# A hybrid attention block: pools that wait tile by tile, later value loads, and a reordered start

## The chip, the cores and the metric

The kernel runs on one core of a Trainium2 chip. The metric is the device time of one execution in microseconds (us); the median of three runs before the change is 946.88 us (944.96 to 947.32). The engines are TensorE (PE, with its weight loads shown apart as PEld), VectorE (DVE), ScalarE (ACT), GpSimd (POOL) and SyncE (SP), which here issues every DMA. Each engine works through its own instructions in the order in which they stand.

## The reference

Input x has 1024 rows of 1024 float32 values. It is normalized and projected onto 6152 columns; these feed two attention branches, two gate paths and a merge:

```python
h = rms_norm(x, g_pre[l], NORM_EPS)
proj = jnp.einsum('bsd,dn->bsn', h, w_in[l])
qa, ka, va, fa, za, qb, kb, vb, zb, gates = jnp.split(proj, SPLIT_POINTS, axis=-1)
...
ya = fox_attention(split_heads(qa, FOX_HEADS), split_heads(ka, FOX_HEADS),
                   split_heads(va, FOX_HEADS), log_f)
ya = merge_heads(ya) * jax.nn.silu(za)
qd = apply_rope(...); kd = apply_rope(...)
yb = diff_attention(qd, kd, vd, lam)
yb = rms_norm(yb, g_subln[l], SUBLN_EPS) * (1.0 - lam_init)
yb = merge_heads(yb) * jax.nn.silu(zb)
gate_a, gate_b = jnp.split(jax.nn.sigmoid(gates), N_BRANCHES, axis=-1)
merged = (gate_a * jnp.einsum('bsw,wd->bsd', ya, w_branch[l, 0])
          + gate_b * jnp.einsum('bsw,wd->bsd', yb, w_branch[l, 1]))
y = jnp.einsum('bsd,de->bse', merged, w_out[l])
x = x + rms_norm(y, g_post[l], NORM_EPS)
```

The forgetting attention (fox) has 8 heads of 64 and adds a running sum of log forget gates to its logits. The differential attention has 4 heads, each the difference of two softmaxes, with rotated queries and keys (rope). Both are causal.

## The kernel before

Most operands are split in two: a rounded high part (`hi`) and the rest (`lo`), so that a product is three matmuls (hi·hi, hi·lo, lo·hi). A cast makes `hi`, a subtraction makes `lo`.

**Start and value projection** (lines 125 to 223). `g_row` is loaded and spread over 128 partitions by a matmul with ones (`gbc`), and ACT copies the two halves to `g_bc`. `x_block(i)` loads 128 rows of x (`xs`), squares and sums them on ACT, forms the scale `rs` on POOL, multiplies by scale and gain on DVE (`xg`), transposes on PE (`xt`), and splits into `hT`; the first block goes in two halves. `load_wv(k)` loads 128 rows of the value weights (`wvraw`) and splits them into `wvhi` and `wvlo`: casts on POOL, except the first half tile on DVE, and subtractions on DVE. `v_block(i)` multiplies (`pv`), and writes the values to DRAM (`vb_d`, `va_d`).

**Attention** (lines 251 to 651). Eight units follow: 0 to 3 differential, 4 to 7 fox. `unit_proj` projects keys and queries in halves (`pk`, `pq`). In units 0 to 3 `rope` copies the result out of PSUM on ACT (`rawk`, `rawq`), which frees its PSUM buffer, fetches the swapped halves by four DMAs (`swk`, `swq`), and combines them on DVE and POOL (`cosT`, `sinT`); `stack` splits into `KA`, `KB`, `TA`, `TB`. `swapped` makes the exchanged query tiles `X0` and `X1` by two DMAs each. `s_row` multiplies a row block of scores (`Sd`, `Sf`) with `TA`/`TB` and then with `X0`/`X1`, takes the row maximum on DVE (`mxd`, `mxf`), and the exponential on ACT. `av` transposes the probabilities and multiplies by the values `V`, loaded from DRAM, 1 MB for each unit. Projections of the next unit, the gate paths (`pz`), and other work are laid between the groups of a unit as filler. The lambda vectors `lt` are loaded at the beginning of this part.

**Gates, merge, output** (lines 654 on). Gate columns are projected (`pg`, then in a scheme with seven products `x_g`, with operands `T` loaded from DRAM), the branches are multiplied (`pb`), merged, and multiplied by the output weights (`x_o`).

**What sets the order.** The code is traced in program order and a scheduler places the instructions of each engine by a simulated timeline, so a small edit can move rows far from it. Tiles come from pools: a pool of a later part lies over the memory of a closed one. Before the change such a tile waits until the whole earlier pool is done with; PSUM pools as well. A tag with `bufs=n` has n slots that are used in turn.

Of the kernel before, what the change touches and what calls it, by code (L numbers as in the profile page):

```python
# [9 lines left out]
F32 = mybir.dt.float32  # L10
F32R = mybir.dt.float32r
AF = mybir.ActivationFunctionType
ALU = mybir.AluOpType
# [28 lines left out]
def f32(ap):  # L42
    return ap.bitcast(F32)
# [3 lines left out]
def tile_hybrid_block(  # L47
# [71 lines left out]
    with ExitStack() as st:  # L119
# [19 lines left out]
        def load_wv(k):  # L139
            raw = xp.tile([P, 1032], F32, tag="wvraw", name=f"wvraw{k}", bufs=4)  # L140
            nc.sync.dma_start(raw[:, 0:512], w[k * P:(k + 1) * P, VB:VB + 512])
            nc.sync.dma_start(raw[:, 512:1032], w[k * P:(k + 1) * P, VA:VA + 520])
            wv_hi[k] = vw.tile([P, 1032], F32R, name=f"wvhi{k}")
            wv_lo[k] = vw.tile([P, 1032], F32R, name=f"wvlo{k}")
            for a, b in ((0, 512), (512, 1032)):
                if k == 0 and a == 0:
                    nc.vector.tensor_copy(wv_hi[k][:, a:b], raw[:, a:b])
                else:
                    nc.gpsimd.tensor_scalar(
                        wv_hi[k][:, a:b], raw[:, a:b], 1.0, 1.0, op0=ALU.mult, op1=ALU.mult)  # L150
                nc.vector.tensor_tensor(
                    wv_lo[k][:, a:b], raw[:, a:b], wv_hi[k][:, a:b], op=ALU.subtract)

        def x_block(i):
            xs = wpool.tile([P, D], F32, tag="wraw", name=f"xs{i}")
            xg = xp.tile([P, D], F32, tag="xg", name=f"xg{i}", bufs=2)
            ss = small.tile([P, 1], F32, tag="ss", name=f"ss{i}")
            rs = small.tile([P, 1], F32, tag="rs", name=f"rs{i}")
            if i == 0:
                for half, acc in enumerate((rs, ss)):  # L160
                    hs = slice(half * CH, (half + 1) * CH)
                    nc.sync.dma_start(xs[:, hs], x2[0:P, hs])
# [88 lines left out]
    with ExitStack() as st:  # L251
        qk = st.enter_context(tc.tile_pool(name="qk", bufs=2))
        pp = st.enter_context(tc.tile_pool(name="pp", bufs=6))
        ptp = st.enter_context(tc.tile_pool(name="ptp", bufs=3))
        stg = st.enter_context(tc.tile_pool(name="stg", bufs=2))
        pj = st.enter_context(tc.tile_pool(name="pj", bufs=2, space=PSUM))
        sps = st.enter_context(tc.tile_pool(name="sps", bufs=3, space=PSUM))
        tps = st.enter_context(tc.tile_pool(name="tps2", bufs=2, space=PSUM))
        yps = st.enter_context(tc.tile_pool(name="yps", bufs=1, space=PSUM))

# [140 lines left out]
        def swapped(T, m, g, nm):  # L401
# [4 lines left out]
            for a, b in ((UPR, DNR), (DNR, UPR)):  # L406
                nc.sync.dma_start(f32(t[a]), f32(src[b, qs]))
            return t

        def s_row(T, m, i, X, bias, boff, nm):  # L410
# [74 lines left out]
        def unit_attn(u, T):  # L485
# [6 lines left out]
            groups = []  # L492

            def load():
                nc.sync.dma_start(f32(vt), src)
                if not diff:
# [35 lines left out]
            else:  # L532
# [25 lines left out]
                for g in GORD[u]:  # L558
                    for m in range(2):
# [6 lines left out]
                                u == 7 and g in FING)))  # L566
            return load, groups

# [46 lines left out]
        for tk in tasks:  # L615
            tk()
        pend = None
        for u in range(8):
            load, groups = unit_attn(u, T)
            if u == 1:  # L620
# [33 lines left out]
    gw = ExitStack()  # L654
    wx = gw.enter_context(tc.tile_pool(name="wx", bufs=2))
    tmp = gw.enter_context(tc.tile_pool(name="tmp", bufs=8))
    ydp = gw.enter_context(tc.tile_pool(name="ydp", bufs=1))
    xst = ExitStack()
    xps = xst.enter_context(tc.tile_pool(name="xps", bufs=8, space=PSUM))

# [86 lines left out]
    tst = ExitStack()  # L747
    tpool = tst.enter_context(tc.tile_pool(name="tpool", bufs=1))

# [39 lines left out]

    def h_load():  # L790
        for m in (4, 6, 5, 7):
            ts = [tpool.tile([P, 4, CH], F32R, tag=f"T{m}{part}", name=f"T{m}{part}")
                  for part in range(2)]
            for part in range(2):
                nc.sync.dma_start(f32(ts[part]), t_d[m][part])
            h_ops[m] = [[t[:, k, :] for k in range(4)] for t in ts]

# [23 lines left out]

    mpool = gw.enter_context(tc.tile_pool(name="mpool", bufs=1))
    mg = mpool.tile([P, KT, S], F32, name="mg")
# [204 lines left out]
```

## Time and profile before

| | |
|---|---|
| median of three runs | 946.88 us |
| the profiled execution | 945.37 us, span 943.3 us |
| PE busy | 895.5 us (95%) |
| DVE, POOL, ACT busy | 625.4, 489.3, 435.8 us |
| DMA | 136.95 MB, mean 145 GB/s |

The page shows the span from the first to the last instruction; the execution's time is 2.1 us longer. PE is counted busy from the start of a matmul to its modelled end, so a busy PE may still be slow; the granted clock and the spacing of matmuls tell that. A line number is that of the kernel before.

### The profile page before, as it was taken

Reading aid. Unit: us, or ns where it says so; the run is one execution under the profiler, and the core shown is the slowest. Engines: PE = TensorE matmul, PEld = TensorE weight load, DVE = VectorE, ACT = ScalarE, POOL = GpSimd, SP = SyncE. Lnnn points to the kernel's source line nnn. Section 1 sums busy time; section 2 is a strip of 40 time slices with the busy share of each in tenths; the row PEclk is TensorE's granted clock in tenths of the full one; section 3 lists DMA queues with packets and bytes.
Section 4 is the critical chain, followed back from the end, with each engine's and each line's share of the span. In section 5 each row is a group of like instructions: output and inputs, shape, how many; then the busy total and the mean of one; then the engine's idle time right before and its main releaser. Section 6 shows DMA issues by size and latency. Waiting matters only on the chain. (4 is left out here: it accounts for less than half of the span.)

```text
span 943.3 us, 13785 instructions
## 1 busy us (share of the span) xinstructions
PE 895.5 (95%) x4600; PEld 750.5 (80%) x4600; DVE 625.4 (66%) x1180; ACT 435.8 (46%) x862; POOL 489.3 (52%) x461
## 2 busy tenths in 40 slices
PE   7999989999999999999999998899999999999993
PEld 5899868787887888888878887788888888887872
DVE  6731248988767778577767558515868893559766
ACT  3421115575656766465755648524443450324331
POOL 7200024446546448364554566407667436878963
PEclk9999999999999999999999999999999999999997
DMA  9532354424316163444542442496556596211332
GB/s 312 186 129 90 118 151 121 110 74 120 108 42 196 43 181 126 123 125 138 167 151 74 135 151 92 152 404 234 174 176 196 165 351 222 72 40 46 105 118 89
DMA packets 118664, 136.95 MB, mean 145 GB/s; under 512 B 10545, under 2 KB 84273, under 8 KB 117570
## 3 DMA queue, kind: packets, MB, share of 16 engines
q1 hardware_dynamic: 118594, 136.08, 45.6%
q8 instruction: 36, 0.59, 0.3%
q14 instruction: 34, 0.28, 0.1%
HBM read 85.65 MB, written 37.81 MB: 131 GB/s over the span
## 5 line engine op out<-in xcount | busy, mean ns | idle before, releaser
L195 PE MATMUL pv<-wvhi,hT 128*128 128x264 f32 (+2 forms) x384 | 89.6, 326 | 0.4 <-DVE hT L181 0.4
L246 PE MATMUL pk<-hT,hi_k 128*128 128x512 f32 x256 | 84.8, 404 | 4.0 <-DVE KB L298 2.2
L246 PE MATMUL pz<-hT,hi_z 128*128 128x512 f32 x256 | 84.3, 396 | 0.0
L246 PE MATMUL pq<-hT,hi_q 128*128 128x512 f32 x256 | 82.8, 397 | 0.0
L713 PE MATMUL x_o<-wo_op,a_o 128*128 128x512 f32 x336 | 77.9, 391 | 3.6 <-POOL a_o L665 2.3
L846 PE MATMUL pb<-yT,hi_br 128*128 128x512 f32 x256 | 78.5, 389 | 0.0
L713 PEld LDWEIGHTS x_o<-wo_op,a_o 128*128 128x128 f32 x336 | 62.7, 188 | 18.7 <-POOL a_o L665 3.7
L713 PE MATMUL x_g<-T,a_g 128*128 128x512 f32 x336 | 77.5, 389 | 0.0
L713 PEld LDWEIGHTS x_g<-T,a_g 128*128 128x128 f32 x336 | 63.1, 188 | 13.1
L195 PEld LDWEIGHTS pv<-wvhi,hT 128*128 128x128 f32 x384 | 64.7, 191 | 6.3 <-DVE hT L181 0.7
L542 POOL TENSOR_SCALAR Pf<-Pf,lf 128x1024 f32<-128x1024 f32 (+3 forms) x64 | 52.5, 822 | 30.6 <-DVE lf L430 27.5
L428 ACT ACTIVATE Pf<-Pf,mxf 128x1024 f32<-128x1024 f32 (+3 forms) x64 | 49.7, 777 | 31.3 <-DVE mxf L423 28.8
L428 ACT ACTIVATE Pd<-Pd,mxd 128x128 f32<-128x128 f32 (+7 forms) x64 | 49.5, 774 | 30.8 <-DVE mxd L423 29.1
L538 POOL TENSOR_TENSOR cb<-cb,trim 128x128 f32<-128x128 f32 x64 | 30.2, 474 | 61.8 <-DVE mxf L423 44.2
L195 PE MATMUL pv<-wvlo,hT 128*128 128x512 f32 (+2 forms) x192 | 61.9, 325 | 0.0
L512 POOL TENSOR_SCALAR Pd<-Pd,ld 128x128 f32<-128x128 f32 (+7 forms) x32 | 25.5, 798 | 69.7 <-DVE ld L511 37.8
L246 PEld LDWEIGHTS pk<-hT,hi_k 128*128 128x128 f32 x256 | 48.3, 193 | 14.5 <-DVE KB L298 2.4
L713 PE MATMUL x_g<-hT,a_g 128*128 128x512 f32 x252 | 58.6, 389 | 0.0
L454 DVE TENSOR_TENSOR plf<-ptf,phf 128x512 fp32r<-128x512 f32 (+1 forms) x80 | 49.6, 633 | 10.4 <-ACT phf L453 9.8
L846 PEld LDWEIGHTS pb<-yT,hi_br 128*128 128x128 f32 x256 | 48.1, 188 | 10.0
L713 PEld LDWEIGHTS x_g<-hT,a_g 128*128 128x128 f32 x252 | 47.3, 188 | 9.8
L246 PEld LDWEIGHTS pq<-hT,hi_q 128*128 128x128 f32 x256 | 47.5, 189 | 8.9
(248 smaller groups left out, 2424.4 us busy)
## 6 DMA issues: line engine op xcount, KB each, us to landing
t_d<-t SPq DMA_DIRECT2D x32, 256.0 KB, 2.2
T<-t_d SPq DMA_DIRECT2D x8, 1024.0 KB, 14.9
raw<-in_w_in_dram SPq DMA_DIRECT2D x14, 512.0 KB, 4.1
vb_d<-vbs SPq DMA_DIRECT2D x8, 512.0 KB
va_d<-vas SPq DMA_DIRECT2D x8, 512.0 KB, 3.7
raw_k<-in_w_in_dram SPq DMA_DIRECT2D x8, 512.0 KB, 5.3
raw_q<-in_w_in_dram SPq DMA_DIRECT2D x8, 512.0 KB
V<-vb_d SPq DMA_DIRECT2D x4, 1024.0 KB
```

What stands on the lines that cost most here:

```text
L195: nc.tensor.matmul(ps[n], lhsT=hT[hp][k // 4][i // 4][:, k % 4, hs], rhs=wt[k][:, a:b], start=first, stop=(k == KT - 1 and hp == 1))
L246: nc.tensor.matmul(ps, lhsT=a[:, k, :], rhs=hT[h][k // 4][c][:, k % 4, :], start=(k == 0 and a is hi and h == 0), stop=(k == KT - 1 and a ...
L428: nc.scalar.activation(pr[:, 0:n], pr[:, 0:n], AF.Exp, bias=mx[:, len(pcs) - 1:len(pcs)], scale=-1.0, accum_out=le)
L454: nc.vector.tensor_tensor(pl[:, 0:n], pt[:, 0:n], ph[:, 0:n], op=ALU.subtract)
L512: nc.gpsimd.tensor_scalar(p2[:, 0:n], p2[:, 0:n], l2, 1.0, op0=ALU.mult, op1=ALU.mult)
L538: nc.gpsimd.tensor_tensor(diag, diag, trim, op=ALU.add)
L542: nc.gpsimd.tensor_scalar(p1[:, 0:n], p1[:, 0:n], l1, 1.0, op0=ALU.mult, op1=ALU.mult)
L713: nc.tensor.matmul(x[m], lhsT=a[:, ai, k, :], rhs=right[m][bi][k], start=(k == 0 and n == 0), stop=(k == 3 and n == 2))
L846: nc.tensor.matmul(ps, lhsT=a[:, kk, :], rhs=yT[g][h][:, k % 2, sl], start=(k == 0 and a is hi and h == 0), stop=(k == 3 and a is lo))
```

## The change

First, `x0`, the first row block, is loaded ahead of `g_row`. The ones that spread the gain become sqrt(D), so that the row scale is (sum + D·eps)^(−1/2): one addition (for the first block DVE adds both halves and D·eps in one instruction; for the others POOL adds) and one power on POOL, where three and two steps stood. The casts of weight tiles 0 and 1 go to ACT.

Second, the pools of attention, gates and merge get `reuse_waits="tile"`: a tile in reused memory waits for the earlier tiles that lie under it, not for their whole pool. Some pools go to the right end of the memory (`side="right"`).

Third, a unit's V load leaves `load` and is queued directly behind a swap of the query tiles (`tc.issue_after`): for unit 0 the first one, for the others one in the second half of the unit before.

Fourth, the T tiles are allocated in another order than they are loaded in.

```diff
+        x0 = wpool.tile([P, D], F32, tag="wraw", name="xs0")
+        for half in range(2):
+            hs = slice(half * CH, (half + 1) * CH)
+            nc.sync.dma_start(x0[:, hs], x2[0:P, hs])
         nc.sync.dma_start(g_row, g_pre[0:1])
         one1 = vw.tile([1, P], F32, name="one1")
-        nc.gpsimd.memset(one1, 1.0)
+        nc.gpsimd.memset(one1, math.sqrt(D))
...
-                if k == 0 and a == 0:
-                    nc.vector.tensor_copy(wv_hi[k][:, a:b], raw[:, a:b])
+                if k < 2:
+                    nc.scalar.copy(wv_hi[k][:, a:b], raw[:, a:b])
                 else:
                     nc.gpsimd.tensor_scalar(
...
-            xs = wpool.tile([P, D], F32, tag="wraw", name=f"xs{i}")
+            xs = x0 if i == 0 else wpool.tile([P, D], F32, tag="wraw", name=f"xs{i}")
...
                     nc.scalar.activation(xg[:, hs], xs[:, hs], AF.Square, accum_out=acc)
-                nc.gpsimd.tensor_tensor(ss, ss, rs, op=ALU.add)
+                nc.vector.tensor_scalar(ss, ss, rs, D * EPS, op0=ALU.add, op1=ALU.add)
             else:
                 nc.sync.dma_start(xs, x2[i * P:(i + 1) * P, :])
                 nc.scalar.activation(xg, xs, AF.Square, accum_out=ss)
-            rstd_of(rs, ss, D, EPS)
+                nc.gpsimd.tensor_scalar(ss, ss, D * EPS, 0.0, op0=ALU.add, op1=ALU.add)
+
+            nc.gpsimd.tensor_tensor(rs, ss, mhalf[:, 0:1], op=ALU.pow)
...
-        qk = st.enter_context(tc.tile_pool(name="qk", bufs=2))
-        pp = st.enter_context(tc.tile_pool(name="pp", bufs=6))
...
-        pj = st.enter_context(tc.tile_pool(name="pj", bufs=2, space=PSUM))
...
+        qk = st.enter_context(tc.tile_pool(name="qk", bufs=2, reuse_waits="tile"))
+        pp = st.enter_context(tc.tile_pool(name="pp", bufs=6, side="right", reuse_waits="tile"))
+        ptp = st.enter_context(tc.tile_pool(name="ptp", bufs=3, side="right", reuse_waits="tile"))
+        stg = st.enter_context(tc.tile_pool(name="stg", bufs=2, side="right", reuse_waits="tile"))
+        pj = st.enter_context(tc.tile_pool(name="pj", bufs=2, space=PSUM, reuse_waits="tile"))
...
             for a, b in ((UPR, DNR), (DNR, UPR)):
-                nc.sync.dma_start(f32(t[a]), f32(src[b, qs]))
+                lastx[0] = nc.sync.dma_start(f32(t[a]), f32(src[b, qs])).ins
+            if vload:
+                with tc.issue_after(lastx[0]):
+                    vload.pop(0)()
             return t
...
+            def load_v():
+                nc.sync.dma_start(f32(vt), src)
+
             def load():
-                nc.sync.dma_start(f32(vt), src)
...
+            load, load_v, groups = nxt or unit_attn(u, T)
+            nxt = None
+            if u == 0:
+                vload.append(load_v)
...
             for n, (wgt, rws, prd) in enumerate(groups):
+                if n == len(groups) // 2 and u < 7:
+                    nxt = unit_attn(u + 1, T)
+                    vload.append(nxt[1])
...
-    xps = xst.enter_context(tc.tile_pool(name="xps", bufs=8, space=PSUM))
+    xps = xst.enter_context(tc.tile_pool(name="xps", bufs=8, space=PSUM, reuse_waits="tile"))
...
     def h_load():
+
+        ts = {m: [tpool.tile([P, 4, CH], F32R, tag=f"T{m}{part}", name=f"T{m}{part}")
+                  for part in range(2)] for m in (6, 4, 7, 5)}
         for m in (4, 6, 5, 7):
-            ts = [tpool.tile([P, 4, CH], F32R, tag=f"T{m}{part}", name=f"T{m}{part}")
-                  for part in range(2)]
             for part in range(2):
-                nc.sync.dma_start(f32(ts[part]), t_d[m][part])
+                nc.sync.dma_start(f32(ts[m][part]), t_d[m][part])
```

The other pools of these parts (`sps`, `tps2`, `yps`, `wx`, `tmp`, `ydp`, `tpool`, `mpool`) get the same argument.

The scheduler turns this into another order. A row gives the line, the operation, what is written and read (with buffer numbers), and the size; behind the change, line numbers are those of the changed file. On SP, at the beginning of attention, the rows before were:

```order
L228 DMA raw_k_1401<-in_w_in_dram 128x8x128
L572 DMA lt<-in_lambda_q_dram 128x64
L572 DMA lt<-in_lambda_k_dram 128x64
L211 DMA va_d<-vas_1116 128x1024
L572 DMA lt<-in_lambda_q_dram 128x64
L572 DMA lt<-in_lambda_k_dram 128x64
L495 DMA V_1345<-vb_d 128x8x256
L495 DMA V_1912<-vb_d 128x8x256
L228 DMA raw_q_1514<-in_w_in_dram 128x8x128
L287 DMA swk_0_1210<-rawk_0_1208 32x512 x4
L287 DMA swq_0_1255<-rawq_0_1253 32x512 x4
```

And now:

```order
L233 DMA raw_k_1400<-in_w_in_dram 128x8x128
L216 DMA va_d<-vas_1115 128x1024
L233 DMA raw_q_1513<-in_w_in_dram 128x8x128
L292 DMA swk_0_1209<-rawk_0_1207 32x512 x4
L292 DMA swq_0_1254<-rawq_0_1252 32x512 x4
L292 DMA swk_1_1293<-rawk_1_1291 32x512 x4
L412 DMA X0d_0_1349<-TA_1172 64x256 x2
L505 DMA V_1344<-vb_d 128x8x256
L412 DMA X1d_0_1353<-TB_1173 64x256 x2
L292 DMA swq_1_1332<-rawq_1_1330 32x512 x4
```

The four `lt` loads have moved far up, and the first V load from ahead of the rope's swaps to between the swaps X0 and X1; the second V load comes later.

On ACT, at the start of the program (`g_bc` is the spread gain, `hT` the transposed rows), before:

```order
L163 ACTIVATE xg_168,rs_170<-xs_167 128x512
L163 ACTIVATE xg_168,ss_169<-xs_167 128x512
L134 COPY g_bc<-gbc_161 128x512
L134 COPY g_bc<-gbc_164 128x512
L180 CAST hT_88<-xt_0_179 128x4x128
L180 CAST hT_90<-xt_1_187 128x4x128
L167 ACTIVATE xg_222,ss_223<-xs_221 128x1024
```

And now:

```order
L166 ACTIVATE xg_170,rs_172<-xs_157 128x512
L166 ACTIVATE xg_170,ss_171<-xs_157 128x512
L151 CAST wvhi_196<-wvraw_193 128x512
L151 CAST wvhi_196<-wvraw_193 128x520
L138 COPY g_bc<-gbc_164 128x512
L151 CAST wvhi_205<-wvraw_202 128x512
L151 CAST wvhi_205<-wvraw_202 128x520
L138 COPY g_bc<-gbc_167 128x512
L185 CAST hT_88<-xt_0_178 128x4x128
L170 ACTIVATE xg_221,ss_222<-xs_220 128x1024
L185 CAST hT_90<-xt_1_186 128x4x128
```

Two weight casts now stand ahead of each copy of the gain. On PE the first six `pv` matmuls have moved from behind the second half's transposes to ahead of them:

```order
L181 MATMUL xt_0_178<-ident,xg_170 128x128 x4
L200 MATMUL pv_0_338<-wvhi_196,hT_88 128x512
L200 MATMUL pv_0_338<-wvlo_197,hT_88 128x512
L200 MATMUL pv_1_339<-wvhi_196,hT_88 128x256
L200 MATMUL pv_1_339<-wvlo_197,hT_88 128x256
L200 MATMUL pv_2_340<-wvhi_196,hT_88 128x264
L200 MATMUL pv_2_340<-wvlo_197,hT_88 128x264
L181 MATMUL xt_1_186<-ident,xg_170 128x128 x4
L200 MATMUL pv_0_338<-wvhi_196,hT_92 128x512
```

Before, both sets of transposes (`xt_0`, `xt_1`) stood ahead of all `pv` matmuls. From unit 4 on, PE's rows stand in the old order but for a few.

More of the change, by code (lines that the diff above doesn't have):

```diff
@@ L566, in unit_attn @@
                                 u == 7 and g in FING)))
-            return load, groups
+            return load, load_v, groups
         lt = pp.tile([P, 4, 64], F32, tag="P", name="lt")
@@ L617, in tile_hybrid_block @@
         pend = None
+        nxt = None
         for u in range(8):
-            load, groups = unit_attn(u, T)
+            load, load_v, groups = nxt or unit_attn(u, T)
+            nxt = None
+            if u == 0:
+                vload.append(load_v)
             if u == 1:
@@ L654, in tile_hybrid_block @@
     gw = ExitStack()
-    wx = gw.enter_context(tc.tile_pool(name="wx", bufs=2))
-    tmp = gw.enter_context(tc.tile_pool(name="tmp", bufs=8))
-    ydp = gw.enter_context(tc.tile_pool(name="ydp", bufs=1))
+    wx = gw.enter_context(tc.tile_pool(name="wx", bufs=2, side="right", reuse_waits="tile"))
+    tmp = gw.enter_context(tc.tile_pool(name="tmp", bufs=8, side="right", reuse_waits="tile"))
+    ydp = gw.enter_context(tc.tile_pool(name="ydp", bufs=1, side="right", reuse_waits="tile"))
     xst = ExitStack()
-    xps = xst.enter_context(tc.tile_pool(name="xps", bufs=8, space=PSUM))
+    xps = xst.enter_context(tc.tile_pool(name="xps", bufs=8, space=PSUM, reuse_waits="tile"))
     def split(dst, src, eng=nc.vector):
@@ L747, in tile_hybrid_block @@
     tst = ExitStack()
-    tpool = tst.enter_context(tc.tile_pool(name="tpool", bufs=1))
+    tpool = tst.enter_context(tc.tile_pool(name="tpool", bufs=1, reuse_waits="tile"))
     yz = {}
@@ L790, in h_load @@
     def h_load():
+        ts = {m: [tpool.tile([P, 4, CH], F32R, tag=f"T{m}{part}", name=f"T{m}{part}")
+                  for part in range(2)] for m in (6, 4, 7, 5)}
         for m in (4, 6, 5, 7):
[L792 to L793 removed]
             for part in range(2):
[L795 to L796 removed]
+                nc.sync.dma_start(f32(ts[m][part]), t_d[m][part])
+            h_ops[m] = [[t[:, k, :] for k in range(4)] for t in ts[m]]
     def gates_pair(d, order):
@@ L819, in tile_hybrid_block @@
     tst.close()
-    mpool = gw.enter_context(tc.tile_pool(name="mpool", bufs=1))
+    mpool = gw.enter_context(tc.tile_pool(name="mpool", bufs=1, reuse_waits="tile"))
     mg = mpool.tile([P, KT, S], F32, name="mg")
```

10 lines of the change are left out of this document (4 added, 6 removed).

## The prediction

> **What bounds the kernel now.** I read the table of engines first, then the windows by stage, then TensorE's waits, and last the timeline at the places that those named.
>
> ```profile
> span 943.3 us, 13785 instructions
> PE 895.5 (95%) x4600; PEld 750.5 (80%) x4600; DVE 625.4 (66%) x1180; ACT 435.8 (46%) x862; POOL 489.3 (52%) x461
> ```
>
> TensorE (PE) is the bound, so a change pays where PE is idle or slow: 943.3 − 895.5 = 47.8 us idle. The next view cuts the span into stages; its columns are stage, length, PE busy (instructions), granted clock, DMA share, GB/s.
>
> ```profile
> 0.00:14.27 14.27, 7.70 (x19) 1.00 0.86 270
> 14.27:104.00 89.73, 89.73 (x572) 1.00 0.44 157
> 104.00:143.00 39.00, 34.58 (x167) 0.96 0.48 139
> 143.00:180.00 37.00, 34.45 (x163) 0.95 0.48 118
> 180.00:360.00 180.00, 174.43 (x934) 1.00 0.39 110
> 360.00:603.00 243.00, 234.16 (x1348) 0.99 0.39 123
> 603.00:620.00 17.00, 16.09 (x72) 1.00 0.93 361
> 620.00:924.00 304.00, 300.13 (x1319) 1.00 0.52 170
> 924.00:943.30 19.30, 4.19 (x18) 0.69 0.25 96
> ```
>
> Idle by stage: 6.6 before the first dense stretch, none to 104, 4.4 where the value projection hands over to attention, 2.6 and 5.6 in the first four attention units, 8.8 in the other four, 0.9 at the handover to the gates, 3.9 later, 15.1 in the tail. The tail and the last 300 us keep their instructions and nearly their order, so about 20 us can be touched at all, and the 8.8 hardly: PE's order from unit 4 to the end is the old one but for a few rows. The waits name the rest (waiter, what it waited for, us, times, longest).
>
> ```profile
> PE Sd L421 <- DVE mxd L423: 6.1, 11, 1.9
> PE pk L246 <- DVE lo_k L236: 2.0, 1, 2.0
> PE pk L246 <- ACT rawk L283: 1.8, 1, 1.8
> PE pq L246 <- DVE lo_q L236: 0.6, 1, 0.6
> ```
>
> **The change part by part.** Durations come from the profiled execution, whose own time is 945.37 us: 943.3 of span and 2.1 around it. The median of the runs shown is 946.88, 1.5 above it.
>
> *Handover to attention (pool waits by tile, V loads behind a swap).* In the timeline (start, us, engine, line, tiles, and in brackets the idle time before and its releaser) the handover reads so:
>
> ```profile
> 111.37 0.33 SPq L572 DMA_DIRECT2D lt<-in_lambda_q_dram  x1
> 114.67 1.41 SPq L495 DMA_DIRECT2D V<-vb_d  x2
> 117.87 2.37 SPq L228 DMA_DIRECT2D raw_q<-in_w_in_dram  x1
> 120.33 4.68 SPq L287 DMA_DIRECT2D swk<-rawk  x4
> 130.16 0.69 DVE L288 TENSOR_TENSOR rawk<-rawk,cosT 128x512 f32<-128x512 f32 x1 [8.77 <-DMA swk<-rawk]
> 135.84 0.70 PE L246 MATMUL pk<-hT,hi_k 128*128 128x512 f32 x2 [1.76 <-ACT rawk L283]
> 138.59 0.51 PE L246 MATMUL pk<-hT,lo_k 128*128 128x512 f32 x1 [2.04 <-DVE lo_k L236]
> ```
>
> The view of DMA issues of that stretch has the size:
>
> ```profile
> V<-vb_d SPq DMA_DIRECT2D x2, 1024.0 KB
> ```
>
> The rotation halves swk are asked for at 120.33 behind two V loads of 1 MB each and a weight tile, and VectorE (DVE) gets them at 130.16. All that hangs on them is late: rotation, ScalarE's (ACT's) copy that frees the projection's PSUM buffer, and on POOL the cast of unit 1's weights behind the rotation's product, so that lo_k is late too. PE pays 1.76 + 2.04 = 3.80 us. After the change no V load stands ahead of swk. A lone set lands in
>
> ```profile
> DMA to landing us min/median/max: 2.0/4.3/6.5
> ```
>
> 2.0 us at best; with four issues of about 0.6 from 118.2 (the weight tile keeps its place near 117.9) that is 118.2 + 2.4 + 2.0 = 122.6, 7.5 us earlier. PE needs the freed buffer and lo_k at about 134.1; lo_k, done just ahead of 138.59, would be done near 131. The cover is 3 us, so I take all 3.80. Bounds: 3.80 and, if a third of the delay stays, half of it, 1.9. What is late next: V itself, 1 MB behind X0's swap and ahead of X1's and of the next query rotation. In PE's order 28 rows of about 0.23 us (300.13 us by 1319 in the late window) now stand between the first score matmul and the first with X1, some 6 us, against about 3 us for 1 MB at the 361 GB/s of the gates' window. I price that at nothing; with the cover gone it costs one stall of the kind priced next.
>
> A stall also costs clock. Right after these two, pairs of matmuls took 1.06 us that take 0.63 at full clock:
>
> ```profile
> 139.79 1.06 PE L246 MATMUL pk<-hT,hi_k 128*128 128x512 f32 x2
> 142.93 0.63 PE L246 MATMUL pk<-hT,hi_k 128*128 128x512 f32 x2
> 170.02 0.49 PE L421 MATMUL Sd<-KA,TA 128*128 128x256 f32 x1 [1.91 <-DVE mxd L423]
> 170.95 1.05 PE L246 MATMUL pq<-hT,hi_q 128*128 128x512 f32 x2
> ```
>
> The windows give the size: clock 0.96 over 39 us is 39 × 0.04 = 1.6 us of full-clock work lost at the handover, 37 × 0.05 = 1.9 in the next stage. I take 1.5 for the first (bounds 0 and 1.6): with the stalls gone, so is the slow stretch. [...] Handover: −5.3.
>
> *lo_q.* Its 0.6 us wait hangs on a store that was issued behind two lt loads, which had to wait for the old pool's last matmul (lt at 111.37). Without them the store goes some 0.4 us earlier: −0.3 (bounds 0, −0.6).
>
> *First rows.* Before:
>
> ```profile
> 5.60 0.19 POOL L112 TENSOR_SCALAR rs<-ss 128x1 f32<-128x1 f32 x1
> 5.88 0.57 POOL L113 TENSOR_TENSOR rs<-rs,mhalf 128x1 f32<-128x1 f32 x1
> 6.74 0.43 DVE L147 CAST wvhi<-wvraw 128x512 fp32r<-128x512 f32 x1 [6.74 <-DMA wvraw<-in_w_in_dram]
> 7.48 4.99 POOL L149 TENSOR_SCALAR wvhi<-wvraw 128x520 fp32r<-128x520 f32 x5 [1.03 <-DMA wvraw<-in_w_in_dram]
> 8.84 1.10 DVE L151 TENSOR_TENSOR wvlo<-wvraw,wvhi 128x520 fp32r<-128x520 f32 x1
> 8.97 1.11 PE L176 MATMUL xt<-ident,xg 128*128 128x128 f32 x4 [2.98 <-DVE xg L171]
> 14.27 1.22 PE L195 MATMUL pv<-wvhi,hT 128*128 128x512 f32 x2 [0.41 <-DVE hT L181]
> 16.80 0.63 PE L195 MATMUL pv<-wvhi,hT 128*128 128x512 f32 x3
> 19.81 0.69 DVE L151 TENSOR_TENSOR wvlo<-wvraw,wvhi 128x520 fp32r<-128x520 f32 x1
> 21.68 1.08 ACT L180 CAST hT<-xt 128x512 fp32r<-128x512 f32 x2 [4.04 <-PE xt L176]
> ```
>
> x goes out one issue (some 0.4 us) earlier, and the row scale, ready at 5.88 + 0.57 = 6.45 before, loses one POOL step (5.60 to 5.88, 0.28): ready near 5.75. Nothing waits for it then, because the order puts ACT's first weight casts ahead of both copies of g_bc, and the first weight half still lands near 6.7. Step by step on ACT, 0.5 us each (two in 1.08 at 21.68): casts of tile 0 at 6.6 and 7.45 (landing), g_bc's first half at 7.95, two casts, its second half at 9.45 to 10.0. On DVE two subtractions, then xg's first half at 8.65: the first transposes at 9.35, 0.4 **later** than 8.97. Then it turns: POOL's casts no longer run beside DVE, whose 1.10 us there compares with 0.69 at 19.81, and the first six value matmuls no longer stand behind the second transposes. PE runs on from about 11.1 and needs the low part of hT at 13.9; DVE has it by 13.5 against 14.27. So the gap of 0.41 closes, and full speed, reached between 14.27 (two matmuls in 1.22) and 16.80 (three in 0.63), comes perhaps 1 us sooner, worth half of that: −1.0 in all, since behind it PE is busy without a gap to 104 and keeps any shift. Bounds: −2.5 (half of the 6.6 idle, less the 0.8 of later PE work that I hold lost) and +1.5 (the second weight tile lands later than 8.9 and holds g_bc's second half).
>
> *Units 0 to 3.* Every engine's rows are shuffled there. Idle is 2.6 + 5.6 = 8.2 us, with 1.9 of clock, nearly all PE waiting for DVE's row maxima. DVE stood idle 8.77 us ahead of 130.16 and was then busy without relief:
>
> ```profile
> 143.00:180.00 37.00, 33.32 (x73) 0.95 0.48 118
> ```
>
> 33.32 of 37 us (DVE's columns here). With 7.5 us of that idling used, and PE some 5 us earlier at the same rows, DVE is 2 us less behind; that could save the stall at 170.02 with its clock, 1.91 + 1.9, or shift it. I take half: −1.9. Bounds: −6 (most of 8.2) and +4 (a new stall of that size, 3.8).
>
> *Gates.* The first gate matmul waits 0.91 us for DVE's last sum of attention, the last reader in the old pool; by tile, its own PSUM bank has been read before:
>
> ```profile
> 603.91 0.74 PE L246 MATMUL pg<-hT,hi_g 128*128 128x512 f32 x2 [0.91 <-DVE ys L552]
> ```
>
> −0.9 (bounds −0.9, 0). T loads move ahead of the y loads; PE reaches T 30 us later, so nothing. The later pools: a wait of 0.3 at most, nothing.
>
> Sum: −5.3 − 0.3 − 1.0 − 1.9 − 0.9 = −9.4; 945.37 − 9.4 = 936.0.
>
> **The rivals.**
> 1. *DVE takes it back.* Rows come earlier, but DVE's 33.32 of 37 sets the pace to 180, and handover and units 0 to 3 give only 1.0 together: 945.4 − 1.0 − 0.3 − 1.0 − 0.9 = 942.2. For: that share. Against: DVE's chain starts 7.5 us earlier as well.
> 2. *X1 behind V: slower.* Each unit's V load now stands ahead of an X1 swap. If PE comes to that score row before the swap lands, it stalls for about 1.9 and loses as much clock: 3.8 each. Handover, lo_q, start and gates bring 7.5, so from two such stalls it loses; with four of the eight, 945.4 − 7.5 + 15.2 = 953.1. For: eight V loads. Against: the 6 us of rows between.
> 3. *The clock stays.* The slow stretch comes anyway, somewhere in the first 180 us: 936.0 + 1.5 = 937.5. [...] For: at 0 to 14 us the clock reads 1.00 while matmuls are slow, so the record is coarse. Against: the rows at 139.79 and 170.95.
> 4. *More.* Units 0 to 3 lose 6 instead of 1.9: 932.
>
> That the change doesn't do what it says is hardly open: the order shows swk free of V.
>
> **How the numbers follow.** Forecast 0.58, rivals 0.12, 0.05, 0.13 and 0.12. 0.3% of 946.88 is 2.8 us, about what this kernel's measurement can tell: faster means below 944.0, slower above 949.7. Faster: 0.55 of the forecast, 0.08 of rival 1, all of 3 and 4: 0.88. Same: 0.03 + 0.04 = 0.07. Slower: 0.05. Median after: 936.0, without the 1.5 that separates the two times before. The range reaches rivals 1 and 4 and the start's and units' bounds: 930 to 943.
>
> **What would show it.** Right: swk back before 124 us and no PE wait for rawk or lo_k; clock 1.00 from 104 to 143; first gate matmul without a wait; PE dense from about 11 us, not 14.27; ACT's g_bc copies after its casts. Wrong: PE waits for X1 or V; DVE's rope still after 128; first transposes later than 10; waits for mxd longer than 6.1 in all.

## The result

The changed kernel takes 938.57 us (median of four runs, 937.61 to 939.48), the kernel before beside it 947.10 (944.96 to 948.29): the ratio is 0.9912, with a 95% interval of 0.9891 to 0.9933. That is 8.5 us, where 9.4 were forecast from the profiled execution. Run once more, as `e5` below, the ratio was 0.9908 (0.9890 to 0.9927). Ratios count fast executions alone: the profiled one of `e1` (994.41 us, granted clock 0.848) and one of `e2` (1779.58 us) are left out. The profiled execution of the changed kernel took 938.93 us, its span 937.0.

### The profile page after: what moved, and what is told of

It reads as the page before. It is cut to its first block, busy times and chain, and to the rows that moved or that the text cites. A ratio compares the mean times of both kernels' runs of the same rounds, so it can differ in the third digit from the quotient of the medians.

```text
span 937.0 us, 13777 instructions
## 1 busy us (share of the span) xinstructions
PE 894.3 (95%) x4600; PEld 751.3 (80%) x4600; DVE 625.1 (67%) x1180; ACT 439.9 (47%) x866; POOL 490.0 (52%) x456
## 5 line engine op out<-in xcount | busy, mean ns | idle before, releaser
L251 PE MATMUL pk<-hT,hi_k 128*128 128x512 f32 x256 | 82.3, 399 | 2.0 <-DVE KB L303 2.0
L554 POOL TENSOR_SCALAR Pf<-Pf,lf 128x1024 f32<-128x1024 f32 (+3 forms) x64 | 50.5, 791 | 28.9 <-DVE lf L440 24.6
L464 DVE TENSOR_TENSOR plf<-ptf,phf 128x512 fp32r<-128x512 f32 (+1 forms) x80 | 49.8, 634 | 11.1 <-ACT phf L463 10.5
```

The costliest lines, as they stand in the source:

```text
L251: nc.tensor.matmul(ps, lhsT=a[:, k, :], rhs=hT[h][k // 4][c][:, k % 4, :], start=(k == 0 and a is hi and h == 0), stop=(k == KT - 1 and a ...
L464: nc.vector.tensor_tensor(pl[:, 0:n], pt[:, 0:n], ph[:, 0:n], op=ALU.subtract)
L554: nc.gpsimd.tensor_scalar(p1[:, 0:n], p1[:, 0:n], l1, 1.0, op0=ALU.mult, op1=ALU.mult)
```

## The profile after

The table of engines and the windows by stage, with the cuts of the prediction (stage, length, PE busy, PEld, DVE, ACT and POOL busy, granted clock, DMA share, GB/s):

```profile
span 937.0 us, 13777 instructions
PE 894.3 (95%) x4600; PEld 751.3 (80%) x4600; DVE 625.1 (67%) x1180; ACT 439.9 (47%) x866; POOL 490.0 (52%) x456
0.00:14.27 14.27, 7.85 (x19) 4.54 (x20) 7.10 (x11) 7.75 (x15) 5.79 (x17) 1.00 0.86 277
14.27:104.00 89.73, 89.22 (x568) 80.23 (x568) 38.89 (x73) 23.87 (x49) 16.88 (x26) 1.00 0.45 157
104.00:143.00 39.00, 39.00 (x199) 33.29 (x198) 17.96 (x24) 7.90 (x15) 9.02 (x7) 1.00 0.42 121
143.00:180.00 37.00, 34.81 (x161) 27.51 (x161) 31.46 (x73) 21.91 (x47) 20.30 (x17) 0.95 0.61 155
603.00:620.00 17.00, 17.00 (x77) 14.08 (x76) 1.12 (x2) 3.73 (x8) 1.29 (x1) 1.00 1.01 409
```

PE's idle time fell from 47.8 to 42.7 us. The handover, 104 to 143, is now full and at full clock: 39.00 of 39 where 34.58 stood, clock 1.00 where 0.96 stood. The stage from 14.27 to 104, full before, has a hole of 0.5, which alone says little: a later profile of the kernel before (`e11`) has one of 0.65. The handover to the gates has lost its hole, and the stage from 143 to 180 still shows a clock of 0.95.

The waits of PE (waiter, what it waited for, us, times, longest):

```profile
PE Sd L431 <- DVE mxd L433: 3.3, 5, 1.4
PE ft L620 <- DVE fs L611: 2.6, 1, 2.6
PE pk L251 <- DVE KB L303: 2.0, 1, 2.0
```

No wait for `rawk`, `lo_k` or `lo_q` is left, and none for X1 or V has come. The waits for `mxd` (3.3 for 6.1) and `fs` (2.6 for 1.1) differ too, but so do two profiles of one kernel: `mxd` has 5.4 in the changed kernel's second profile, and 7.0 and 5.2 in two more of the kernel before, where `fs` has up to 2.0. The handover in the timeline:

```profile
118.41 2.53 SPq L292 DMA_DIRECT2D swk<-rawk  x4
122.55 0.69 DVE L293 TENSOR_TENSOR rawk<-rawk,cosT 128x512 f32<-128x512 f32 x1 [5.43 <-DMA swk<-rawk]
133.91 0.62 PE L251 MATMUL pk<-hT,hi_k 128*128 128x512 f32 x2
134.37 0.39 PE L251 MATMUL pk<-hT,lo_k 128*128 128x512 f32 x1
597.09 0.68 PE L251 MATMUL pg<-hT,hi_g 128*128 128x512 f32 x2
```

`swk` is issued at 118.41 and DVE has it at 122.55 (130.16 before; 122.6 was forecast), the next key matmuls follow at 133.91 without a gap, and the first gate matmul, in the last row, follows attention without the 0.91 of idling.

The start:

```profile
4.08 3.75 PE L137 MATMUL gbc<-g_row,one 1*128 1x512 f32 x4 [4.08 <-DMA g_row<-in_g_pre_dram]
7.95 0.58 ACT L138 COPY g_bc<-gbc 128x512 f32<-128x512 f32 x1
9.49 1.11 PE L181 MATMUL xt<-ident,xg 128*128 128x128 f32 x4 [1.67 <-DVE xg L176]
11.28 0.79 PE L200 MATMUL pv<-wvhi,hT 128*128 128x512 f32 x1 [0.68 <-ACT hT L185]
13.96 1.22 PE L200 MATMUL pv<-wvhi,hT 128*128 128x512 f32 x2
22.23 2.12 DVE L176 SCALAR_TENSOR_TENSOR xg<-xs,rs,g_bc 128x512 f32<-128x512 f32 x2 [0.46 <-POOL rs L173]
25.00 0.66 PE L181 MATMUL xt<-ident,xg 128*128 128x128 f32 x4 [0.30 <-DVE hT L186]
25.42 1.09 PE L200 MATMUL pv<-wvlo,hT 128*128 128x512 f32 x2
```

Up to 14 us it goes as forecast: first transposes at 9.49 (9.35), dense from 11.28 (11.1), the low part of `hT` met at 13.96 without a gap (14.27 before). Then the third row block comes late: DVE scales it at 22.23 (20.42 before) after waiting for POOL's `rs`, PE waits 0.30 for its low part at 25.00, and the two matmuls at 25.42 take 1.09, where two of that shape take 0.63.

One execution of each kernel is not enough to say where 8.5 us went, because executions of the same kernel differ by 3 us and more (the kernel before here: 944.96 to 948.29). In the experiments the kernel before was profiled twice more, and the changed one once more. The stages below are cut at PE's own rows (first or last matmul of a tile), so that a shift stays with the stage that made it:

| stage, cut at | before, three profiles | changed, two | difference of means | forecast |
|---|---|---|---|---|
| start to first `pq` | 116.7, 117.9, 115.9 | 117.6, 117.6 | +0.8 | −1.0 |
| first `pq` to last `ypd` (handover, units 0 to 3) | 267.2, 267.5, 268.8 | 260.5, 260.6 | −7.3 | −7.5 |
| last `ypd` to last `ypf` (units 4 to 7) | 218.8, 220.4, 220.1 | 218.9, 217.3 | −1.7 | 0 |
| last `ypf` to first `x_g` (gates) | 23.1, 23.1, 23.1 | 21.9, 22.0 | −1.2 | −0.9 |
| first `x_g` to last `x_o` | 302.1, 302.3, 301.9 | 302.8, 302.6 | +0.6 | 0 |
| last `x_o` to the end | 15.4, 15.3, 15.4 | 15.3, 15.4 | 0 | 0 |
| span | 943.3, 946.5, 945.2 | 937.0, 935.5 | −8.8 | −9.4 |

The widest stage can be cut once more, at the first `ypd`. From the first `pq` to there it took 46.6, 47.2 and 46.7 us before and 40.9 and 40.4 in the changed kernel, 6.2 less for nearly the same work (179 or 180 matmuls on record before, 182 after); the rest of the stage gave 1.1.

The rows behind the widest of these stages, from the changed kernel's first profile (matmuls, their count, ns least/median/most, first to last):

```profile
L251 PE MATMUL pq<-hT,hi_q x256: 387/389/632, 117.6 to 500.0; 128*128 128x512 f32 x128
L484 PE MATMUL ypd<-pld,V x80: 273/280/415, 159.9 to 378.1; 128*128 128x256 f32 x64, 128*128 128x128 f32 x16
```

## The experiments

Ratios are to the kernel before on the same chip, with their 95% intervals. Theory A is each time what the traces had shown by then; its rivals stand beside it. The edits are shown in short.

**The new start alone** (`e1`, and again `e12`). The kernel before with this part of the change:

```diff
+        for half in range(2):
+            nc.sync.dma_start(x0[:, hs], x2[0:P, hs])
         nc.sync.dma_start(g_row, g_pre[0:1])
...
-                if k == 0 and a == 0:
-                    nc.vector.tensor_copy(wv_hi[k][:, a:b], raw[:, a:b])
+                if k < 2:
+                    nc.scalar.copy(wv_hi[k][:, a:b], raw[:, a:b])
...
+            nc.gpsimd.tensor_tensor(rs, ss, mhalf[:, 0:1], op=ALU.pow)
```

> The kernel before with the first part of the change alone (x asked for first, the scale in two steps, the casts of weight tiles 0 and 1 on ACT). Theory A, from the traces: in the changed kernel the first key matmul behind the value projection starts at 112.11 us against 111.18, so this part costs 0.9 us there: value projection's end near 112.1, time about +0.9 us (946.3 beside 945.4). Rival, the prediction: 1.0 us earlier, end near 110.2, time -1.0. The stalls of the handover stay under both (rawk 1.8 and lo_k 2.0, each within 0.5).

> The first experiment's kernel again (new start alone), since its profile fell on a stretch of lowered clock and its stages cannot be read. Three profiles of the kernel before put the first query projection at 115.9 to 117.9 us and the last ypd matmul 267.2 to 268.8 us behind it. Theory A (the start alone costs, 0.5 to 1.5 us): first query projection at 117.6 as in both profiles of the changed kernel, the stretch behind it 267 to 269, time some 1 us above before. Rival F: the 2.3 us that it lost in time come from the shuffled rows of units 0 to 3, so the stretch takes 269.5 or more.

Measured: 1.0024 (1.0008 to 1.0040), and the second time 1.0014 (0.9996 to 1.0032): 2.3 and 1.3 us more, not less, though the second interval reaches below 1. The profile of `e12` puts the first `pq` at 117.8 and the last `ypd` 267.6 behind it, as theory A had it; rival F is out. The handover stalls stayed:

```profile
PE pk L251 <- DVE lo_k L241: 2.0, 1, 2.0
PE pk L251 <- ACT rawk L288: 1.3, 1, 1.3
```

So this part brings nothing by itself; the best estimate, from the two ratios, is a loss of one or two us.

**Later V loads alone** (`e2`).

```diff
             for a, b in ((UPR, DNR), (DNR, UPR)):
-                nc.sync.dma_start(f32(t[a]), f32(src[b, qs]))
+                lastx[0] = nc.sync.dma_start(f32(t[a]), f32(src[b, qs])).ins
+            if vload:
+                with tc.issue_after(lastx[0]):
+                    vload.pop(0)()
...
             def load():
-                nc.sync.dma_start(f32(vt), src)
```

> The kernel before with the third part alone: V loads behind a swap of the query tiles, pools as before. Theory A: the V loads ahead of swk are the whole cause of the late rotation, so swk is back before 125 us, no wait for rawk or lo_k, and what the changed kernel gains between the first query projection and the end of unit 3 (about 7 us by the traces) comes here too: time -6 to -7 us, the waits for lo_q (0.6) and of the first gate matmul (0.9) stay. Rival B: the pool waits hold the handover as well (tiles of attention wait for the whole pools of the value projection), so V alone brings at most half, -3 or less, and a wait for rawk or lo_k of over 1 us is still there.

**Pools by tile alone** (`e3`).

```diff
-        qk = st.enter_context(tc.tile_pool(name="qk", bufs=2))
+        qk = st.enter_context(tc.tile_pool(name="qk", bufs=2, reuse_waits="tile"))
...
-        pj = st.enter_context(tc.tile_pool(name="pj", bufs=2, space=PSUM))
+        pj = st.enter_context(tc.tile_pool(name="pj", bufs=2, space=PSUM, reuse_waits="tile"))
```

> The kernel before with the second and fourth parts alone: pools wait tile by tile, T allocated in the other order, V loads where they were, ahead of swk. Theory A: the first gate matmul no longer waits (-0.9), nor lo_q (-0.3 to -0.6), the stalls for rawk and lo_k stay near 3.8 in all: time -1 to -1.5 us. Rival B: with pools that wait by tile the V loads are issued early enough (from 114.67 to some 2 us sooner) that swk lands by 126 and the stalls go without the move of V: -4 us or more.

**Both, with the old start** (`e4`): the diff is the two together.

> The changed kernel without its first part: old start, pools by tile, V behind the swap. Theory A: the first part costs about 0.9 us that nothing later gives back, so this kernel ends about 0.9 us sooner than the changed one: some 937.7 beside 938.6, value projection's end near 111.2. Rival, the prediction: it ends 1.0 us later, 939.6. Rival C: DVE and the row maxima absorb the shift of the first 100 us, so that both end within 0.3 us of each other.

| | ratio | first `pq` | to last `ypd` | to last `ypf` | to first `x_g` |
|---|---|---|---|---|---|
| before (means) | 1 | 116.8 | 267.8 | 219.8 | 23.1 |
| V later | 0.9935 (0.9915 to 0.9956) | 116.9 | 264.3 | 216.3 | 23.1 |
| pools by tile | 0.9950 (0.9931 to 0.9970) | 117.5 | 262.1 | 218.6 | 21.9 |
| both | 0.9926 (0.9906 to 0.9945) | 116.4 | 263.2 | 215.9 | 21.9 |
| all (changed, means) | 0.9912, 0.9908 | 117.6 | 260.6 | 218.1 | 22.0 |

Each part brings most of the gain alone, 6.1 and 4.7 us of 945.34, and together they bring 7.0, not 10.8. The handover's stall is one and the same for both. By stages it is less even: up to the last `ypd`, V later gains 3.5 us, the pools 5.7, both 4.6 and the whole change 7.3. The first three are one profile each; the waits for X1 below are part of it, the rest is open. So theory A of `e2` held for the waits and the time, but not for the 7 us in this stage. With V later, the `lt` loads still wait for the old pool, but no V stands between them and `swk` (SP's and DVE's timeline):

```profile
113.73 0.78 SPq L579 DMA_DIRECT2D lt<-in_lambda_k_dram  x1
118.52 2.53 SPq L287 DMA_DIRECT2D swk<-rawk  x4
123.54 0.69 DVE L288 TENSOR_TENSOR rawk<-rawk,cosT 128x512 f32<-128x512 f32 x1 [4.51 <-DMA swk<-rawk]
```

With the pools by tile, and both V loads still ahead of `swk`:

```profile
110.75 1.00 SPq L495 DMA_DIRECT2D V<-vb_d  x2
118.32 2.53 SPq L287 DMA_DIRECT2D swk<-rawk  x4
123.08 1.78 DVE L288 TENSOR_TENSOR rawk<-rawk,cosT 128x512 f32<-128x512 f32 x1
```

In the second, V goes out at 110.75 instead of 114.67, since no `lt` load stands ahead of it that waits for the old pool. A V load lands 9.3 us after its issue, so the last is in near 120.5, some 2 us behind `swk`'s first issue. One more row moved with the pools: the weight tile `raw_q`, issued ahead of `swk` at 117.87 before, now goes out behind it, at 123.19. No run separates the earlier V from the later weight tile. Theory A of `e3`, that the stalls stay, was wrong, and its rival right: 0.2 is left of the wait for `rawk`, and 0.7 for `rawq` is new. What cannot be shared stays with its part: the gates' 1.2 us come only where the pools wait by tile (21.9 against 23.1), and with V alone the 0.9 for `ys` and the 0.5 for `lo_q` are still there:

```profile
PE pg L246 <- DVE ys L559: 0.9, 1, 0.9
PE Sd L427 <- DMA X1d<-TB: 1.0, 1, 1.0
PE pq L246 <- DVE lo_q L236: 0.5, 1, 0.5
```

The middle row is the prediction's rival 2 in small: behind the V load, X1 came 1.0 us late, once. It came in `e4` (0.7) and `e7` (0.9) too, but in neither profile of the changed kernel. Of `e4`'s theories none held whole: without the new start the first `pq` comes 1.2 us earlier than in the changed kernel, but units 0 to 3 then take 2.6 longer, and the first `x_g` starts at 617.4 against 618.9 and 617.5. By time the two cannot be told apart. Rival C had the outcome; its mechanism, that DVE's row maxima absorb the shift, was not shown, since the rows of those units stand in another order in the two kernels.

**Which part of the start** (`e5` to `e7`, on one chip). `e5` is the changed kernel. `e6` puts its casts back:

```diff
-                if k < 2:
-                    nc.scalar.copy(wv_hi[k][:, a:b], raw[:, a:b])
+                if k == 0 and a == 0:
+                    nc.vector.tensor_copy(wv_hi[k][:, a:b], raw[:, a:b])
```

`e7` takes the old start back but for the scale in two steps:

```diff
-        for half in range(2):
-            nc.sync.dma_start(x0[:, hs], x2[0:P, hs])
         nc.sync.dma_start(g_row, g_pre[0:1])
...
-                if k < 2:
-                    nc.scalar.copy(wv_hi[k][:, a:b], raw[:, a:b])
+                if k == 0 and a == 0:
+                    nc.vector.tensor_copy(wv_hi[k][:, a:b], raw[:, a:b])
```

> The changed kernel itself, to stand beside the next three on the same chip. Theory A (the new start costs about 1.1 us and nothing later gives it back): ratio to before 0.991 to 0.994, value projection's end (first key matmul) at 112.1 us.

> The changed kernel with its weight casts where they were (first half tile on DVE, the others on POOL); x first and the scale in two steps stay. In its order the third row block's load (xs) stands behind the sixth weight tile's on SP, and its scale behind that tile's casts on POOL, as in the changed kernel. Theory A: that is what costs the start its time (PE loses about 1.3 us between 20 and 27 us waiting for DVE's third block and weight parts), so here too value projection ends at 112 or later, and the time is that of the changed kernel within 0.5 us. Rival B: the casts on ACT cost it, because both copies of the gain stand behind them; then it ends at 111 or earlier and the time is 1 us lower.

> The changed kernel with the old start but for the scale in two steps (x behind g_row, casts as before). Here the third block's load stands ahead of the sixth weight tile, as before. Theory A: value projection ends at 110.6 to 111.0 (111.2 before, less up to 0.3 for the POOL step that is left out), time 1.0 to 1.5 us below the changed kernel. Rival B says the same of this kernel; rival C, that DVE's row maxima absorb a shift of the first 100 us, says within 0.4 us of the changed kernel at the end.

Measured: `e5` 936.90 us, 0.9908 (0.9890 to 0.9927); `e6` 938.41, 0.9924 (0.9902 to 0.9946); `e7` 936.22, 0.9900 (0.9878 to 0.9922). Value projection ended (first key matmul) at 112.1, 114.5 and 110.6. Rival B fell: without ACT's casts the start is not 1 us earlier but 2.4 later; of theory A the end came true, the time, 1.5 us higher, not within its 0.5, though the intervals overlap. DVE then takes a cast and both subtractions, 1.09 for one beside POOL's casts, ahead of the first `xg`:

```profile
7.53 0.43 DVE L151 CAST wvhi<-wvraw 128x512 fp32r<-128x512 f32 x1 [2.17 <-DMA wvraw<-in_w_in_dram]
9.20 1.09 DVE L155 TENSOR_TENSOR wvlo<-wvraw,wvhi 128x520 fp32r<-128x520 f32 x1 [0.52 <-POOL wvhi L153]
10.22 1.10 DVE L176 SCALAR_TENSOR_TENSOR xg<-xs,rs,g_bc 128x512 f32<-128x512 f32 x1
11.37 1.11 PE L181 MATMUL xt<-ident,xg 128*128 128x128 f32 x4 [3.73 <-DVE xg L176]
```

So ACT's casts help once x comes first, and what costs is x first with the order that it brought. `e6` and `e7` differ in that alone: value projection ends 3.9 us apart, of which 3.4 stand already at the first transposes (11.37 against 8.01): with x first, DVE casts the first weight half at 7.53 instead of 6.14, and one subtraction more stands ahead of `xg`. The third row block's load and scale, now behind the sixth weight tile's, may come on top; no run moves them alone. With the scale alone (`e7`) that block stands ahead again, and value projection ends 1.5 us earlier than in the changed kernel; the time, 0.7 us lower, does not separate the two.

**A start with the order put right** (`e8`, `e9`). `e8` is `e7` with the first half weight tile cast on ACT and DVE's subtractions of that tile held behind both halves of `xg`:

```diff
-                    nc.vector.tensor_copy(wv_hi[k][:, a:b], raw[:, a:b])
+                    nc.scalar.copy(wv_hi[k][:, a:b], raw[:, a:b])
...
+            if k == 0:
+                with tc.issue_after(lastg[0]):
+                    load_wv(k)
```

`e9` casts both halves on ACT, behind the gain's copies (`lastg`), and also holds the second tile's subtractions behind the low part of the first half of `hT` (`hl`):

```diff
-                if k == 0 and a == 0:
-                    nc.vector.tensor_copy(wv_hi[k][:, a:b], raw[:, a:b])
+                if k == 0:
+                    nc.scalar.copy(wv_hi[k][:, a:b], raw[:, a:b])
...
         x_block(0)
         for k in range(KT):
-            load_wv(k)
+            if k == 0:
+                with tc.issue_after(lastg), tc.issue_after(ahead["xg"][1]):
+                    load_wv(k)
+            elif k == 1:
+                with tc.issue_after(ahead["hl"][0]):
+                    load_wv(k)
+            else:
+                load_wv(k)
```

> The kernel of the run before, with two edits at the start: the first half weight tile is cast on ACT, and on DVE the first tile's subtractions are held behind both halves of the first block's xg. Theory A: rows ready early are worth what they save on PE: first transposes near 6.9 us (8.97 before, 9.49 in the changed kernel), value projection's end near 109.2, time 2 us below the kernel with the scale alone. Rival D: PE is then fed by the weight tiles, which land every 1.5 us or so until 16 us, and not by the rows: transposes at 6.9, but value projection's end at 110.4 or later, time within 0.7 us of the kernel with the scale alone.

> The kernel with xg ahead of the subtractions, taken further: both halves of the first weight tile are cast on ACT behind the gain's copies, and on DVE the second tile's subtractions are held behind the low part of the first half of hT, for which PE waited 1.85 us at 13.29. Theory A (PE can be fed sooner once the order on DVE is right): that wait is gone, value projection ends at 108.5 to 109.5, 1 to 2 us before the 110.4 of the kernel before it, time 1 to 1.5 us lower (about 934). Rival D (the weight parts, two per tile at 1.0 us each on DVE beside POOL's casts, feed PE): the wait only moves behind the second tile, value projection ends at 110.0 or later, time within 0.5 us.

Measured: `e8` 935.26 us, 0.9893 (0.9874 to 0.9913), and `e9` 933.68, 0.9874 (0.9846 to 0.9903). In `e8` the first transposes came at 7.16, but PE then waited for the low part of `hT`, which stood behind four subtractions of 4.17 us on DVE, and value projection ended at 110.4, as rival D had it; the time, 1.0 us below `e7`'s, lies between the two theories. In `e9` that wait is gone and PE is fed from 8.92 on, but for 0.24 and 0.56. `e8`'s timeline:

```profile
8.46 4.17 DVE L151 TENSOR_TENSOR wvlo<-wvraw,wvhi 128x512 fp32r<-128x512 f32 x4
13.29 0.74 PE L198 MATMUL pv<-wvhi,hT 128*128 128x512 f32 x2 [1.85 <-DVE hT L184]
```

And `e9`'s:

```profile
7.13 1.97 PE L180 MATMUL xt<-ident,xg 128*128 128x128 f32 x8 [1.01 <-DVE xg L174]
8.92 0.80 PE L200 MATMUL pv<-wvhi,hT 128*128 128x512 f32 x1
17.55 1.29 PE L180 MATMUL xt<-ident,xg 128*128 128x128 f32 x8 [0.56 <-DVE xg L174]
```

Value projection ended at 109.7, between what the two theories said; the time is near theory A's 934. By the medians this kernel beats the one before by 11.2 us of 944.83. Against the changed kernel, on another chip, the gain is 3 us by the ratios, and the intervals just overlap.

**The clock behind a stall** (`e10`, `e11`): the kernel before, unchanged, profiled twice more.

> The kernel before, profiled once more. Theory A, of the prediction (a stall of near 2 us costs clock as well): behind the stalls for rawk and lo_k pairs of matmuls take 1.06 us again, the granted clock of 104 to 180 us is 0.95 or 0.96 again. Rival E (a slow stretch comes by chance; the changed kernel's two profiles had three more and none more of them at the same waits): the stalls are there again (1.8 and 2.0 within 0.4), the clock behind them may be 1.00.

> The same once more, so that three profiles of the kernel before stand beside each other. Theory A: slow pairs behind the same two stalls in all three. Rival E: in some, not in others.

The stalls came again (1.87 and 2.04, 1.43 and 2.06), and behind them the slow pairs, so theory A held at this place, in three of three profiles and in `e12`'s. In all nine profiles of kernels without these stalls the clock reads 1.00 from 104 to 143. But the two stalls make 3.3 to 3.9 us together, with 0.7 us of work between them, so this place does not tell whether one stall of 2 us is enough. From `e10`:

```profile
137.21 0.70 PE L246 MATMUL pk<-hT,hi_k 128*128 128x512 f32 x2 [1.87 <-ACT rawk L283]
139.96 0.80 PE L246 MATMUL pk<-hT,lo_k 128*128 128x512 f32 x1 [2.04 <-DVE lo_k L236]
140.55 1.06 PE L246 MATMUL pk<-hT,hi_k 128*128 128x512 f32 x2
```

Elsewhere rival E held. Nearly all the kernels have one stall in common, of about 2 us for `KB` near 490 us. In the changed kernel's first profile a slow stretch follows it, in its second none (timelines of the first, then of the second):

```profile
483.34 0.85 PE L251 MATMUL pk<-hT,hi_k 128*128 128x512 f32 x2 [1.99 <-DVE KB L303]
484.42 1.05 PE L251 MATMUL pk<-hT,hi_k 128*128 128x512 f32 x2
485.70 1.05 PE L251 MATMUL pk<-hT,hi_k 128*128 128x512 f32 x2
486.98 0.73 PE L251 MATMUL pk<-hT,hi_k 128*128 128x512 f32 x2
```

```profile
482.79 0.73 PE L251 MATMUL pk<-hT,hi_k 128*128 128x512 f32 x2 [2.06 <-DVE KB L303]
483.59 0.63 PE L251 MATMUL pk<-hT,hi_k 128*128 128x512 f32 x2
484.28 0.62 PE L251 MATMUL pk<-hT,hi_k 128*128 128x512 f32 x2
```

## Why the prediction was right, and where it was off

**Handover, −5.3, and units 0 to 3, −1.9, with lo_q −0.3.** Together −7.5; measured −7.3 between the first `pq` and the last `ypd`. The step that carried it, `swk` back at 122.6 and with it no stall for `rawk` and `lo_k`, was met to 0.05 us, and no later wait took its place. Up to the first `ypd` it is −6.2, where −5.6 were forecast, and behind it −1.1 for −1.9. That 1.9 was half of a price, a choice, so it is partly luck that the sum came out to 0.2. One sentence of the step was too narrow: it laid the whole stall to the V loads standing ahead of `swk`. In the experiment with the pools alone V still stands there, 4 us earlier, and the stall is gone; either part suffices for that.

**The clock term, 1.5 of it.** At the handover the clock was met: 0.96, 0.95 and 0.91 in three profiles before, 1.00 in both after. The two stalls there stand too close together to tell whether one of them alone costs clock; behind the single wait of about 2 us for `KB` a slow stretch came in eight of twelve profiles, and in four it did not. The step from the handover to "with the stalls gone, so is the slow stretch" was too strong for the rest of the program. Rival 3, a slow stretch that comes anyway in the first 180 us, is in the first profile after, behind a wait of 1.44 us, and not in the second, behind the same wait (timelines of the first, then of the second):

```profile
162.63 0.56 PE L431 MATMUL Sd<-KA,TA 128*128 128x512 f32 x1 [1.44 <-DVE mxd L433]
163.41 1.06 PE L251 MATMUL pq<-hT,hi_q 128*128 128x512 f32 x2
```

```profile
162.07 0.50 PE L431 MATMUL Sd<-KA,TA 128*128 128x512 f32 x1 [1.44 <-DVE mxd L433]
173.29 0.50 PE L431 MATMUL Sd<-KA,TA 128*128 128x512 f32 x1 [0.55 <-DVE mxd L433]
175.30 0.44 PE L431 MATMUL Sd<-KA,TA 128*128 128x384 f32 x1 [0.80 <-DVE mxd L433]
```

Yet the stage pays nothing for it: from the first `pq` to the last `ypd` it is 260.5 us in the first and 260.6 in the second, in which PE waited for `mxd` at 173 and 175 as it did not in the first. So where rival 3 came, its price of 1.5 was not paid. The spans, 937.0 and 935.5, differ in units 4 to 7, by 1.6.

**Gates, −0.9.** −1.2, and only with the pools by tile.

**Start, −1.0.** This is the term that failed, in its sign: +0.8 at the first `pq`, and 1.3 to 2.3 us more time when done alone; with the rest of the change in place (`e4`) the time shows no loss. The steps to 14 us were right to 0.2 us, but full speed came 0.3 us sooner (the first single `pv` of 512 columns that takes about 0.4 us instead of 0.63 comes at 16.22 for 16.56), where about 1 was forecast, and their base was a late one: the first transposes, at 8.97 in the profile before, came at 8.26 and 8.20 in two more. The step that failed is "behind it PE is busy without a gap to 104 and keeps any shift": the order beyond the rows that the prediction looked at had moved as well. On SP the third block's load now stands behind the sixth weight tile's, on POOL its scale behind that tile's casts, and PE pays between 20 and 26 us. In the three profiles with the new start a transpose waits for DVE's low part (0.30, 0.3 and 0.2 us), and value projection ends at 112.1, 112.1 and 112.3. That speaks for the third block, though no run moves it alone. The bound of +1.5 held the term.

**What was priced at nothing.** Units 4 to 7 gave 1.7 in the mean. About half is luck with the clock: all three profiles before have a slow stretch behind the wait for `KB` near 490 us (218.8 to 220.4 in this stage), of the two after one has it (218.9) and one not (217.3). The other kernels without the handover's stalls agree: 217.6 to 218.1 with it, 215.9 to 216.3 without (the pools alone, where PE has no such wait, took 218.6). For the rest, some 0.9, no cause was found. From the first `x_g` on 0.6 was lost, for which no cause was found either.

**The base.** The forecast, 936.0, lies 2.6 us under 938.57. Of these 0.9 are the gain, 8.5 for 9.4: the start's 1.8 and the 0.6 behind the gates were missing, the 1.7 of units 4 to 7 came unasked, so that the near miss is partly luck. The other 1.7 are the base: the sum started from an execution of 945.37, while the four beside the changed kernel had a median of 947.10. Such an execution is nothing rare, for on the four chips of the experiments the same kernel's medians were 944.83 to 945.60; but the forecast was for the time beside the median shown, and for that, leaving out the 1.5 was the wrong choice.

Rivals 1 and 4 did not come, and rival 2 only as waits of 0.7 to 1.0 us in three of the experiments.

## What to carry to other kernels

A load that a pool's wait holds back also holds what stands behind it on its queue, here 2 MB of V from 110.75 to 114.67: look for the small transfer that is late, and ask both who stands ahead of it and what that one waits for, since mending either can be enough, and mending both then pays once. Where a scheduler places the rows, follow a part's effect some 20 us past the last row that was meant to move. And when a change is worth less than 1%, cut the stages at the program's own rows and take more than one profile before giving each stage its share.

## What the runs showed of the hardware

A stall of about 2 us may or may not cost clock. Behind the wait for `KB`, which ends between 479.3 and 492.8 us, the clock fell in eight of twelve profiles (waits of 1.93 to 2.36 us) and held in four (1.92 to 2.06), the same kernel on both sides; so between 1.9 and 2.1 us the length of the stall does not decide. What does decide, no run shows. In the rows above from the changed kernel's first profile the slow stretch lasts about 3.4 us: the granted clock reads 0.50 from 483.8 to 487.2, a pair takes 1.05 us for 0.63, and the work behind it comes some 1.6 us later: from the stall to the last `pq` it is 17.0 us in the first profile of the changed kernel (483.34 to 500.3) and 15.3 in the second (482.79 to 498.1). In the first profile of the kernel before, the stretch behind the same wait is as long: the clock reads 0.50 from 491.0 to 494.4.

The start of one and the same program varies by 2 us: in three profiles of the kernel before the first `pq` came at 116.7, 117.9 and 115.9 (between these in three more kernels with the old start), in three with the new one between 117.6 and 117.8. Before, it goes with how far PE was at 20 us: the records have 48, 40 and 60 matmuls to there.
